# Dividing three more pairs of forget heads ahead of their turns, a third causal addition on GpSimd, and the turns of head group A five steps earlier

## The chip, the cores and the metric

One core of one Trainium2 chip runs the whole program. The metric is the device time of one execution in microseconds (us). The kernel before takes 1001.78 us, the median of three runs from 1001.54 to 1001.94. The engines are named as in the profile: PE (TensorE, matrix products), PEld (its weight loads), DVE (VectorE), ACT (ScalarE), POOL (GpSimd), SP (which issues most DMAs).

## The reference

Two layers work on 256 tokens of width 1024. Each layer is `h += 1/2 SwiGLU(norm(h))`, then `h += mixer(norm(h))`, then `h += 1/2 SwiGLU(norm(h))` again, all in float32. The mixer is where the change lies:

```python
proj = u @ w_in                       # 256 x 3792, split into the inputs of three head groups
aq = rope(rms(aq)); ak = rope(rms(ak))     # A: 4 query heads, one key/value head
iq, ik = rope(iq), rope(ik)                # A: indexer, 8 heads: the top 64 keys of each query
bq = rope(rms(bq)); bk = rope(rms(bk))     # B: 4 heads; with 256 tokens plain causal attention
cq, ck = rms(cq), rms(ck)                  # C: 8 heads
log_f = log_sigmoid(cf + forget_bias); c = cumsum(log_f)
s = q @ k.T / 8 (+ c_q - c_k in group C); masked softmax(s) @ v
o_c = o_c * sigmoid(cg)
out = concat(o_a, o_b, o_c) @ w_out
```

## The kernel before

Every float32 weight is split into a high and a low part (`wh`, `wl`), and a product is made of three PE products of parts. ACT makes `wh` (line 126), DVE makes `wl = raw - wh` (line 130); `W.pump()` asks for both of the next unit, `W.high()` and `W.low()` for one of them. Eight units are held at most, so the splits run ahead of PE.

The mixer's projection goes in chunks (`iq, ib, b, a, ck, cq, cv, cg`) of four units each. After each unit PE's instructions of one **step** stand in the program (12 products of 128x512), and `run_side()` then emits whatever has been put down for that step with `at_step(n, ...)`. In this way attention's small work is laid between the projection's products. Engines work through their own lists in order; what another engine must have made first is waited for. `A_ROOT`, `A_TURN`, `SUMS_STEP` and their like are such step numbers. A fraction counts for the next whole step: 21.3 is emitted after step 22, and 28.5 after step 29.

For group A, `a_norm` (at `A_ROOT`, step 22) takes the sums of squares on DVE, raises them to -1/2 on POOL (`y_a`, line 351), and scales the key head on POOL (`akd`, line 720). POOL has four things in a row there: `y_ck` and two scalings of `cka` (asked for at step 21), then `y_a` and the two `akd`. `a_turn` (at `A_TURN`) then turns the four query tiles `aqr` and the two `akd` on PE into PSUM (line 970), and ACT copies them to `aT`. `cumsum` turns the log gates `lf` on PE (line 905) and sums them on DVE; `sums_out` and `sums_in` send the sums through DRAM to every partition (`tab`, `laterkT`, `laterlater`), and `causal_part` adds the causal mask to them.

A pair of heads goes through `scores` (s, PE), `masks` (m, DVE: adds the mask and finds the row's extreme), `exps` (e, ACT), `roots` (n, DVE: reciprocals of the row sums), `flip` (F or f, PE: turns the 12 blocks of probabilities by products with the identity, line 180), `spread` (y: copies the turned blocks from PSUM to SBUF, half on DVE or ACT and half on ACT, line 193), `values` (v, PE) and `outT` (o). There are two ways to divide by the row sums. Pairs in `divided` scale the probabilities themselves before the flip (`divide`, words D or d, two instructions for a head). The others spread the reciprocals over a tile (`wide`, line 1112), turn that too with four more PE instructions, copy it with the blocks, and multiply afterwards. A letter string gives the order: `EARLY` after step 30, `AC_ORDER` after the projection. In it pairs 0 and 1 are group A, pairs 2 to 5 are group C; `h`, `r`, `p`, `x` stand for the output projection with `w_out`, and `j` is `W.low()`.

Names in rows: `ps_gu` and `ps_acc` are the two sets of four PSUM banks, `xhl` the normalized input in two parts, `oh`/`ol` and `ohl` the heads' outputs in two parts, `pT` turned probabilities, `cT` turned queries, keys and gates of group C.

Of the kernel before, what the change touches and what calls it, by code (L numbers as in the profile page):

```python
# [10 lines left out]
F32 = mybir.dt.float32  # L11
# [3 lines left out]
ALU = mybir.AluOpType  # L15
# [3 lines left out]
P = 128  # L19
S = 256  # L20
D = 1024
# [5 lines left out]
TOPK = 64  # L27
# [10 lines left out]
WARM = 6  # L38
BRIDGE = 3
P_BUFS = 4  # L40
EARLY = "S Q q m0 e0 m1 e1 m2 e2 b0 b1 m3 j B0 B1 e3"
AC_ORDER = """
    h0 n0 d0 C n1 d1 d2 d3 T c0 F0 k0 F1 y0 y1 c1 k1 s2 v0 v1 m4 m5 g o0 o1 e4 e5 s3 s4
    h1 m6 m7 w2 e6 e7 l q q n2 n3 w3 m8 m9 h2 h3
    F2 f3 y2 y3 s5 v2 v3 e8 e9 m10 m11 e10 e11 o2 o3 n4 j
    r0 r1 n5 j F4 F5 y4 y5 h4 j v4 v5 o4 o5 j
    p h5 h6 h7 Z r2 N p r3 p r4 p M x2 p x3 p
"""
B_TURN, A_ROPE, B_STEP, A_ROOT, A_TURN, SUMS_STEP, TOP_STEP, A_STEP = 18, 18, 20, 21.3, 28.5, 21, 15, 30


CHUNKS = [
# [102 lines left out]
def kernel(ctx: ExitStack, tc: tile.TileContext, x, ffn1_norm, ffn1_w_gate, ffn1_w_up, ffn1_w_down,  # L155
# [10 lines left out]
    at = ctx.enter_context(tc.tile_pool(name="at", bufs=1))  # L166
# [5 lines left out]
    V, A, G, T = nc.vector, nc.scalar, nc.gpsimd, nc.tensor  # L172

    def bank(tag):
        return psum.tile([P, 512], F32, name="ps_" + tag, tag=tag)
# [6 lines left out]
    def turned(ps, dst, copies):  # L182
        for e, copy in enumerate(copies):
            d = dst[..., 64 * e:64 * e + 64]
            n = 64
            for k in d.shape[1:-1]:
                n *= k
            src = ps[e][:, :n]
            if len(d.shape) == 3:
                src = src.rearrange("p (b j) -> p b j", j=64)  # L190
            else:
                src = src.rearrange("p (a b j) -> p a b j", a=d.shape[1], j=64)
            copy(d, src)
# [4 lines left out]
    def tmp(n):  # L198
        return tp.tile([P, 512], F32, name="tmp", tag="tmp")[:, :n]
# [39 lines left out]
    W = Weights(tc, raw_pool, split_pool)  # L239
# [89 lines left out]
    causal = cp.tile([P, 3 * P], F32, name="causal")  # L329
# [12 lines left out]
    def mm3(o, lhs, rhs, start, stop):  # L342
        mm(o, lhs[0], rhs[0], start, False)
        mm(o, lhs[0], rhs[1], False, False)
        mm(o, lhs[1], rhs[0], False, stop)
# [344 lines left out]
    def mixer(l, norm, nxt):  # L690
        side, count = [], itertools.count()
        step = [0]

        def at_step(n, fn):
            side.append((n, next(count), fn))

        def run_side():
            due = sorted(x for x in side if x[0] <= step[0])
            for x in due:
                x[2]()  # L700
            side[:] = [x for x in side if x[0] > step[0]]
# [47 lines left out]
        st = {}  # L749
# [44 lines left out]
        def post_ib(ps):  # L794
# [10 lines left out]
            for t in range(2):  # L805
                x = small[t][:, None, 0:64]
# [24 lines left out]
                A.activation(la, la, AF.Ln, bias=1.0)  # L831
                A.activation(small[0][:, 0:1], ones[:, 0:1], AF.Exp)

            at_step(SUMS_STEP - 3, log_sigmoid)
            def forget():
                V.scalar_tensor_tensor(lf, fg, 0.0, la, op0=ALU.min, op1=ALU.subtract)

            at_step(SUMS_STEP - 2, forget)
            st["ikT"] = at.tile([P, 1, S], F32, name="ikT", tag="qs")

            def turn_ik():
# [42 lines left out]
                V.match_replace(out=st["score"][t], in_to_replace=m8, in_values=st["score"][t], imm_value=-3e38)  # L884

            def amask_begin():
                st["amask"] = at.tile([P, 3 * P], F32, name="amask", tag="amask")
                G.tensor_copy(st["amask"][:TOPK, 0:P], causal[:TOPK, 0:P])

            at_step(A_STEP - 4, amask_begin)  # L890

            def amask():
                am, score = st["amask"], st["score"]
                for d, x in ((am[:, P:], score[1]), (am[TOPK:, :P], score[0][TOPK:])):
                    V.tensor_scalar(d, x, -2e38, NEG, op0=ALU.is_gt, op1=ALU.mult)

            at_step(A_STEP - 0.5, amask)

            for r in range(TOPK // 8):
                at_step(TOP_STEP + 2 * r, lambda: topk(1))  # L900
# [20 lines left out]
                    nc.sync.dma_start(to, bass.AP(tensor=src.tensor, offset=src.offset + h * S,  # L921
                                                    ap=[[0, P], [S, k], [1, n]]))

            at_step(SUMS_STEP + 1, cumsum)
            at_step(SUMS_STEP + 3, sums_out)
            at_step(SUMS_STEP + 5, sums_in)
            for i in range(2):
                at_step(A_STEP - 2, lambda i=i: causal_part(i))

        def causal_part(i):  # L930
            x = st["first"][:, 2 * i:2 * i + 4] if i % 2 == 0 else st["later"][i // 2][:, :, 1]
            (V if i > 1 else G).tensor_tensor(x, x, causal[:, None, 0:P].to_broadcast([P, 4, P]), op=ALU.add)

        def post_a(ps):
            ss = sm.tile([P, 2, 5], F32, name="ssa", tag="ss")
# [40 lines left out]
        def post_b(ps):  # L976
# [34 lines left out]
            def qk_b(kind, h):  # L1011
                return st["bT"][:, h // 2 * 2], st["bT"][:, h // 2 * 2 + 1]

            st["B"] = run_heads([("B", h) for h in range(4)], qk_b, lambda i, fn: at_step(B_STEP + i, fn))

        c_ss = at.tile([P, 2, 2, 8], F32, name="c_ss", tag="c_ss")
# [35 lines left out]
        def tanh():  # L1052
            ps, hr = st.pop("cg"), st["hr"]
            sg = at.tile([P, 2, 512], F32, name="sg", tag="sg")
            for t in range(2):
                A.activation(sg[:, t], ps[t], AF.Tanh, scale=hr[:, t:t + 1])
            st["sg"] = sg
            for _ in range(2):
                bank("gu")


        def run_heads(hs, qk, emit=None):
            pj, pt, op, sums, bs, wide, flipped, gated, high = {}, {}, {}, {}, {}, {}, {}, {}, {}
            divided = range(2)
            blocks = ((slice(0, P), slice(0, P), slice(0, P)), (slice(P, 3 * P), slice(P, S), slice(0, S)))
            tag = "acc" if emit else "gu"

# [65 lines left out]
            def spread(p):  # L1133
                both = pp.tile([P, 8, P], F32, name="pT", tag="pT", bufs=2)
                kind, h = hs[2 * p]
                turned(flipped.pop(p), both[:, :6] if p in divided else both,
                       (A.copy if emit else V.tensor_copy, A.copy))
                pt[p] = [both[:, 3 * e:3 * e + 3].rearrange("p a b -> p (a b)") for e in range(2)]
                gated[p] = both[:, 6:8].rearrange("p a b -> p (a b)")
                if kind == "C":  # L1140
                    o = st["gate"][:, h // 2]
                    if p not in divided:
                        o = tmp(S)
                        G.tensor_tensor(o, gated[p], st["gate"][:, h // 2], op=ALU.mult)
                    gated[p] = o
# [36 lines left out]
            if emit is None:  # L1182
                return scores, masks, exps, roots, divide, flip, spread, values, outT
# [10 lines left out]

        hs = [("A", h) for h in range(4)] + [("C", h) for h in range(8)]
        scores, masks, exps, roots, divide, flip, spread, values, outT = run_heads(hs, qk_ac)

        def c_T(ps, src, g, at):
# [5 lines left out]
        def both_scores(_):  # L1204
# [8 lines left out]
            for p in range(2):  # L1213
                b_values(p, st["keys"][p][:, S:])

        todo = dict(S=both_scores, D=divide, d=lambda i: divide(i, V), s=scores, m=masks, e=exps, n=roots, F=flip, y=spread, v=values, o=outT,
                    Q=lambda _: W.high(), q=lambda _: W.high(), j=lambda _: W.low(),
                    b=lambda p: st["B"][1](p), B=lambda p: st["B"][2](p), T=lambda _: tanh(), w=causal_part)

        def do(text):  # L1220
            for word in text.split():
                todo[word[0]](int(word[1:] or 0))

        at_step(A_STEP, lambda: do(EARLY))

        oT = {}
        posts = dict(ib=post_ib, a=post_a, b=post_b, ck=post_ck, cq=post_cq, cv=post_cv, cg=post_cg)
        index_queries()
        for name, cols in CHUNKS[1:]:
            n = sum(c[1] for c in cols)  # L1230
            ps = [bank("gu") for _ in range(2)]
            for u in range(4):
                w = W.take()
                for kk in range(2):
                    k = 2 * u + kk
                    for t in range(2):
                        ts = slice(t * P, (t + 1) * P)
                        mm3(ps[t][:, :n], (norm.h[:, k, ts], norm.l[:, k, ts]), [v[:, kk] for v in w],
                            k == 0, k == KT - 1)
                step[0] += 1  # L1240
                run_side()
                if step[0] < A_STEP and step[0] != 8:
                    W.pump()
            posts[name](ps)
            if step[0] == 8:
                W.pump(2)
# [70 lines left out]
        def norm_out(_):  # L1317
# [5 lines left out]
            for t in range(2):  # L1323
# [3 lines left out]
                    p=lambda _: W.pump(), Z=residuals, N=norm_T, M=norm_out)  # L1327
# [23 lines left out]
    for l in range(DEPTH):  # L1351
        norm = ffn(norm, lambda: Norm(1, l), lambda: before_mixer(l), l == 0)
        norm = mixer(l, norm, lambda: Norm(2, l))
        norm = ffn(norm, (lambda: Norm(0, l + 1)) if l + 1 < DEPTH else None)
# [37 lines left out]
```

## Time and profile before

| what | value |
|---|---|
| median of the runs | 1001.78 us |
| the profiled execution's own time | 1001.55 us |
| its span, first to last instruction | 999.8 us |
| PE busy | 995.5 us |
| DVE, ACT, POOL busy | 799.3, 597.4, 162.0 us |

The time outside the span is 1.75 us. A profile's row of PE shows a pipelined product: its length is longer than the time until the next can start, so starts are compared, not lengths. The two mixers run from about 189 to 321 us and from 684 to 816 us; the second repeats the first 494.9 us later, so rows of the first stand for both.

### The profile page before, as it was taken

The page shows a single profiled execution, that of the slowest core. Times are in us where ns is not written, and L with a number is a line of the kernel's source. Part 1 is how long each engine was busy: PE and PEld are TensorE (multiplying, and loading weights), DVE is VectorE, ACT ScalarE, POOL GpSimd, SP SyncE. Part 2 cuts the span into 40 slices and gives each one's busy share as a digit, 9 for nine tenths or more (in the row PEclk, how much of TensorE's full clock was granted, in tenths as well). Part 3 has the DMA queues.
Part 4 walks back from the last instruction along what each step waited for, and adds up shares of the span by engine and source line. Part 5 has one row for each costly group of instructions (what it writes and reads, how often), then busy time and mean ns, then how long its engine had stood idle before and what let it go on. Part 6 is the DMA issues. An engine that isn't in the chain of part 4 may idle for free.

```text
span 999.8 us, 15219 instructions
## 1 busy us (share of the span) xinstructions
PE 995.5 (100%) x5692; PEld 856.5 (86%) x5692; DVE 799.3 (80%) x1482; ACT 597.4 (60%) x1118; POOL 162.0 (16%) x188
## 2 busy tenths in 40 slices
PE   9999999999999999999999999999999999999998
PEld 8888888888878888888888888889888788888887
DVE  5978778789998777777888777787899977777775
ACT  6655555597786555555465555556968765555552
POOL 2003000058812000000000020001677210000000
PEclk9999999999999999999999999999999999999999
DMA  9865647475725555555655655565566164464731
GB/s 291 274 224 160 224 156 238 129 238 188 230 87 169 173 164 193 187 195 196 199 169 176 207 183 198 185 208 166 192 211 232 58 208 159 140 238 148 232 128 43
DMA packets 133498, 184.80 MB, mean 185 GB/s; under 512 B 7152, under 2 KB 106800, under 8 KB 133424
## 3 DMA queue, kind: packets, MB, share of 16 engines
q1 hardware_dynamic: 133392, 183.82, 56.2%
q8 instruction: 45, 0.74, 0.3%
q14 instruction: 29, 0.24, 0.1%
q10 hardware_dynamic: 32, 0.01, 0.0%
HBM read 182.75 MB, written 1.06 MB: 184 GB/s over the span
## 4 chain that ended last, share of the span: by engine, by line
PE 98%; DMA 1%; SPq 0%; ACT 0%; issue 0%; DVE 0%
PE ps_gu L340 66%; PE ps_acc L340 30%; PE ps_acc L180 1%; DMA raw<-in_ffn_w_up_dram 1%; PE ps_acc L375 1%; PE ps_gu L180 1%; SPq L100 0%; SPq L225 0%; PE ps_gu L375 0%; PE ps_acc L970 0%; ACT wh L126 0%; PE ps_acc L402 0%; PE ps_acc L844 0%; PE ps_acc L905 0%; DVE trunk L419 0%
## 5 line engine op out<-in xcount | busy, mean ns | idle before, releaser
L130 DVE TENSOR_TENSOR wl<-raw,wh 128x1024 fp32r<-128x1024 f32 (+2 forms) x342 | 421.6, 1240 | 27.1 <-ACT wh L126 27.1
L126 ACT CAST wh<-raw 128x1024 fp32r<-128x1024 f32 (+2 forms) x341 | 341.2, 1037 | 14.4 <-PE ps_acc L340 7.7
L340 PE MATMUL ps_gu<-xhl,wh 128*128 128x512 f32 (+1 forms) x1472 | 347.6, 388 | 0.2 <-ACT wh L126 0.2
L340 PEld LDWEIGHTS ps_gu<-xhl,wh 128*128 128x128 f32 x1472 | 272.5, 188 | 54.4 <-ACT wh L126 0.7
L340 PEld LDWEIGHTS ps_gu<-xhl,wl 128*128 128x128 f32 x1472 | 187.5, 191 | 4.1 <-DVE wl L521 0.2
L340 PE MATMUL ps_gu<-xhl,wl 128*128 128x256 f32 (+1 forms) x1472 | 190.3, 282 | 0.0
L484 DVE TENSOR_TENSOR tmp<-ps_gu,tmp 128x256 f32<-128x256 f32 x176 | 72.8, 422 | 109.3 <-ACT tmp L483 109.0
L340 PE MATMUL ps_acc<-wh,hh 128*128 128x512 f32 (+1 forms) x352 | 137.3, 390 | 0.0
L340 PE MATMUL ps_acc<-wl,hh 128*128 128x512 f32 (+1 forms) x352 | 137.0, 389 | 0.0
L340 PE MATMUL ps_acc<-wh,hl 128*128 128x512 f32 (+1 forms) x352 | 136.6, 388 | 0.0
L340 PE MATMUL ps_gu<-wh,xhl 128*128 128x512 f32 (+2 forms) x448 | 133.4, 375 | 0.0
L483 ACT COPY tmp<-ps_gu 128x256 f32<-128x256 f32 x176 | 63.4, 371 | 92.1 <-PE ps_gu L340 91.9
L498 ACT CAST hh<-tmp 128x256 fp32r<-128x256 f32 x80 | 32.6, 407 | 120.2 <-DVE tmp L495 120.2
L340 PEld LDWEIGHTS ps_gu<-wh,xhl 128*128 128x128 f32 x448 | 82.5, 188 | 14.1 <-issue 1.7
L490 ACT ACTIVATE tmp<-tmp 128x256 f32<-128x256 f32 x88 | 36.9, 419 | 82.7 <-DVE tmp L488 82.5
L340 PE MATMUL ps_gu<-wl,xhl 128*128 128x512 f32 (+2 forms) x224 | 83.2, 372 | 0.0
L351 POOL TENSOR_TENSOR y_n<-msq,minus_half 128x2 f32<-128x2 f32 x6 | 7.0, 1174 | 441.9 <-DVE msq L350 441.9
L340 PEld LDWEIGHTS ps_acc<-wh,hl 128*128 128x128 f32 x352 | 66.1, 188 | 13.9
L340 PEld LDWEIGHTS ps_acc<-wh,hh 128*128 128x128 f32 x352 | 66.2, 188 | 12.6
L340 PEld LDWEIGHTS ps_acc<-wl,hh 128*128 128x128 f32 x352 | 66.3, 188 | 12.3 <-DVE wl L130 0.2
L340 PEld LDWEIGHTS ps_gu<-wl,xhl 128*128 128x128 f32 x224 | 42.2, 188 | 5.9
L508 DVE TENSOR_TENSOR tmp<-tmp,rb 128x256 f32<-128x256 f32 x88 | 37.7, 428 | 3.0
(237 smaller groups left out, 901.5 us busy)
## 6 DMA issues: line engine op xcount, KB each, us to landing
raw<-in_ffn_w_down_dram SPq DMA_DIRECT2D x44, 1024.0 KB, 5.0
raw<-in_ffn_w_gate_dram SPq DMA_DIRECT2D x42, 1024.0 KB, 6.9
raw<-in_ffn_w_up_dram SPq DMA_DIRECT2D x42, 1024.0 KB, 7.8
raw<-in_w_in_dram SPq DMA_DIRECT2D x24, 1024.0 KB, 5.1
raw<-in_w_out_dram SPq DMA_DIRECT2D x8, 1024.0 KB, 5.0
raw<-in_w_in_dram SPq DMA_DIRECT2D x4, 768.0 KB, 5.0
raw<-in_w_in_dram SPq DMA_DIRECT2D x4, 656.0 KB, 4.2
raw<-in_ffn_w_gate_dram SPq DMA_DIRECT2D x3, 512.0 KB, 7.5
```

The source lines that it names most:

```text
L126: self.nc.scalar.copy(hv, src)
L130: (engine or self.nc.vector).tensor_tensor(lv, self.srcs[self.n_low], hv.bitcast(F32), op=ALU.subtract)
L180: T.transpose(b[:, 64 * i:64 * i + 64], src[r], ident[r, r])
L340: T.matmul(o, l, r, start=start, stop=stop, skip_group_check=True)
L351: G.tensor_tensor(y, dst, minus_half[:, :n], op=ALU.pow)
L375: T.transpose(ps[:, i, t * P:(t + 1) * P], trunk[:, t, (2 * mp + i) * P:(2 * mp + i + 1) * P], ident)
L483: A.copy(o, ps[:, 1])
L484: V.tensor_tensor(o, ps[:, 0], o, op=ALU.add)
L490: A.activation(th, t_, AF.Tanh, scale=0.5)
L498: (V.tensor_copy if late else A.copy)(hh, t_)
L508: V.tensor_tensor(t_, t_, norm.rb, op=ALU.mult)
```

## The change

Six things change. (1) `divided` grows from two pairs to five: pairs 2, 3 and 4 (forget heads) now have their probabilities divided before the flip, head 4 on POOL (new word G), heads 5 to 9 on DVE (d); their reciprocals are no longer spread, turned and copied, and the gate is multiplied in directly. (2) `a_turn` moves from step 29 to step 24, `cumsum` from step 22 to 24, `sums_out` from 24 to 26, `sums_in` from 26 to 27. (3) The mask of group A and the causal additions move from steps 28 and 30 to the word `a` in `EARLY`; three additions instead of two go to POOL, and they read a copy of the mask that DVE makes in `amask`. (4) In `spread`, group B's copies go to DVE and ACT instead of ACT twice. (5) Step 29 asks for a `wh` only, and its `wl` follows as `j` in `EARLY`. (6) `AC_ORDER` is reordered around this; the second `j` of its fourth line stands two places later, and mask 9 after the copies of pairs 2 and 3.

```diff
-EARLY = "S Q q m0 e0 m1 e1 m2 e2 b0 b1 m3 j B0 B1 e3"
+EARLY = "S j a Q q m0 e0 m1 e1 m2 e2 b0 b1 m3 j B0 B1 e3"
...
-    h1 m6 m7 w2 e6 e7 l q q n2 n3 w3 m8 m9 h2 h3
-    F2 f3 y2 y3 s5 v2 v3 e8 e9 m10 m11 e10 e11 o2 o3 n4 j
-    r0 r1 n5 j F4 F5 y4 y5 h4 j v4 v5 o4 o5 j
+    h1 m6 m7 n2 G4 d5 e6 e7 l q q n3 d6 d7 w3 m8 h2 h3
+    F2 f3 y2 y3 m9 s5 v2 v3 e8 e9 m10 m11 e10 e11 o2 n4 d8 d9 o3 n5
+    r0 r1 j F4 F5 y4 y5 h4 j v4 v5 o4 o5 j j
...
-B_TURN, A_ROPE, B_STEP, A_ROOT, A_TURN, SUMS_STEP, TOP_STEP, A_STEP = 18, 18, 20, 21.3, 28.5, 21, 15, 30
+B_TURN, A_ROPE, B_STEP, A_ROOT, A_TURN, SUMS_STEP, TOP_STEP, A_STEP = 18, 18, 20, 21.3, 24, 24, 15, 30
...
             def amask():
                 am, score = st["amask"], st["score"]
-                for d, x in ((am[:, P:], score[1]), (am[TOPK:, :P], score[0][TOPK:])):
+                for d, x in ((am[:, P:3 * P], score[1]), (am[TOPK:, :P], score[0][TOPK:])):
                     V.tensor_scalar(d, x, -2e38, NEG, op0=ALU.is_gt, op1=ALU.mult)
-
-            at_step(A_STEP - 0.5, amask)
+                V.tensor_copy(am[:, 3 * P:], causal[:, 0:P])
+                for i in range(3):
+                    causal_part(i)
+
+            st["mask"] = amask
...
-            at_step(SUMS_STEP + 1, cumsum)
-            at_step(SUMS_STEP + 3, sums_out)
-            at_step(SUMS_STEP + 5, sums_in)
-            for i in range(2):
-                at_step(A_STEP - 2, lambda i=i: causal_part(i))
+            at_step(SUMS_STEP, cumsum)
+            at_step(SUMS_STEP + 2, sums_out)
+            at_step(SUMS_STEP + 3, sums_in)
...
-            (V if i > 1 else G).tensor_tensor(x, x, causal[:, None, 0:P].to_broadcast([P, 4, P]), op=ALU.add)
+            late = i > 2
+            mask = causal[:, 0:P] if late else st["amask"][:, 3 * P:]
+            (V if late else G).tensor_tensor(x, x, mask[:, None].to_broadcast([P, 4, P]), op=ALU.add)
...
-            divided = range(2)
+            divided = range(5)
...
-                       (A.copy if emit else V.tensor_copy, A.copy))
+                       (V.tensor_copy, A.copy))
...
-                if step[0] < A_STEP and step[0] != 8:
+                if step[0] < A_STEP - 1 and step[0] != 8:
                     W.pump()
+                if step[0] == A_STEP - 1:
+                    W.high()
```

On PE, the turns of group A stood at the end of step 29 in the kernel before, 84 products after the turns of the log gates:

```order
L340 MATMUL ps_gu<-wh,xhl 128x512
L970 MATMUL ps_acc<-ident,aqr 128x128 [waits Pool_49] x2
L970 MATMUL ps_acc<-ident,aqr 128x128 x2
L970 MATMUL ps_acc<-ident,akd_2514 128x128 [waits Pool_49]
L970 MATMUL ps_acc<-ident,akd_2515 128x128 [waits Pool_49]
L340 MATMUL ps_gu<-wh,xhl 128x512
```

In the changed kernel both sets of turns stand together on PE, at the end of step 24:

```order
L340 MATMUL ps_gu<-wh,xhl 128x512
L908 MATMUL ps_acc<-ident,lf 8x128 [waits DVE_49]
L908 MATMUL ps_acc<-ident,lf 8x128
L973 MATMUL ps_acc<-ident,aqr 128x128 [waits DVE_49,Pool_49]
L973 MATMUL ps_acc<-ident,aqr 128x128 [waits Pool_49]
L973 MATMUL ps_acc<-ident,aqr 128x128 x2
L973 MATMUL ps_acc<-ident,akd_2514 128x128 [waits DVE_49,Pool_49]
L973 MATMUL ps_acc<-ident,akd_2515 128x128 [waits Pool_49]
L340 MATMUL ps_gu<-wh,xhl 128x512 [waits Activation_49]
```

The turns of `akd` still wait for POOL, and everything that PE has to do later stands behind them. The turns of `lf` came down by two steps (24 products), those of `aqr` and `akd` went up by five.

On POOL, the rows that make `akd` stand in the changed kernel exactly as they stood, behind the scaling of `cka`:

```order
L351 TENSOR_TENSOR y_ck<-c_ss,minus_half 128x16 [waits DVE_49]
L720 TENSOR_TENSOR cka_130<-cka_130,y_ck 128x512 [waits Activation_49,Pool_49]
L720 TENSOR_TENSOR cka_131<-cka_131,y_ck 128x512 [waits Activation_49]
L351 TENSOR_TENSOR y_a<-ssa,minus_half 128x10 [waits DVE_49]
L720 TENSOR_TENSOR akd_2514<-ak_2512,y_a 128x128 [waits PE_49,Pool_49]
L720 TENSOR_TENSOR akd_2515<-ak_2513,y_a 128x128 [waits PE_49]
```

Nothing on POOL moved ahead of them or away from ahead of them; what it does later (three additions, the division of head 4) follows.

On PE again, the flips of pairs 2 and 3 and the scores of pair 5 in the kernel before, in AC_ORDER (`tmp` is the spread reciprocal):

```order
L180 MATMUL ps_gu<-ident,p 128x64 x3
L180 MATMUL ps_gu<-ident,tmp 128x64 [waits DVE_49]
L180 MATMUL ps_gu<-ident,tmp 128x64 x3
L180 MATMUL ps_acc<-ident,p 128x64 [waits Activation_49] x2
L180 MATMUL ps_acc<-ident,p 128x64 x10
L180 MATMUL ps_acc<-ident,tmp 128x64 [waits DVE_49]
L180 MATMUL ps_acc<-ident,tmp 128x64 x3
L340 MATMUL ps_gu<-cT 128x128 [waits DVE_49] x2
```

And the end of the same stretch on PE in the changed kernel:

```order
L180 MATMUL ps_acc<-ident,p 128x64 [waits DVE_49]
L180 MATMUL ps_acc<-ident,p 128x64
L180 MATMUL ps_acc<-ident,p 128x64 [waits DVE_49]
L180 MATMUL ps_acc<-ident,p 128x64 x3
L340 MATMUL ps_gu<-cT 128x128 [waits DVE_49]
L340 MATMUL ps_gu<-cT 128x128 [waits Activation_49]
```

The turns of `tmp` are gone. The second product of the scores now waits for ACT: its PSUM bank is the one that ACT's copy of pair 2 (line 193) sets free, where before both banks came free by masks on DVE.

## Rows read from the trace of the kernel before

**Rows 1.** The page: span, and busy time of each engine.

```profile
span 999.8 us, 15219 instructions
PE 995.5 (100%) x5692; PEld 856.5 (86%) x5692; DVE 799.3 (80%) x1482; ACT 597.4 (60%) x1118; POOL 162.0 (16%) x188
```

**Rows 2.** All waits of PE: total us, times, longest.

```profile
PE ps_gu L340 <- POOL minus_half L219: 1.0, 1, 1.0
PE ps_gu L340 <- ACT wh L126: 0.2, 1, 0.2
```

**Rows 3.** Timeline of PE, end of step 22: start, us, then the instruction.

```profile
250.34 0.38 PE L905 MATMUL ps_acc<-ident,lf 128*8 128x128 f32 x2
250.47 0.48 PE L340 MATMUL ps_gu<-wh,xhl 128*128 128x512 f32 x1
```

**Rows 4.** Timeline of PE, the turns of group A.

```profile
269.63 0.60 PE L970 MATMUL ps_acc<-ident,aqr 128*128 128x128 f32 x4
270.07 0.38 PE L970 MATMUL ps_acc<-ident,akd 128*128 128x128 f32 x2
```

**Rows 5.** Timeline of POOL, 251 to 259 us; [idle before, and who ended it].

```profile
251.16 2.91 POOL L351 TENSOR_TENSOR y_ck<-c_ss,minus_half 128x16 f32<-128x16 f32 x1 [4.68 <-DVE c_ss L350]
254.15 2.09 POOL L720 TENSOR_TENSOR cka<-cka,y_ck 128x512 f32<-128x512 f32 x2
256.20 1.95 POOL L351 TENSOR_TENSOR y_a<-ssa,minus_half 128x10 f32<-128x10 f32 x1
258.23 0.76 POOL L720 TENSOR_TENSOR akd<-ak,y_a 128x128 f32<-128x128 f32 x2
```

**Rows 6.** Line 351: ns min/median/max, first and last start in us.

```profile
L351 POOL TENSOR_TENSOR y_n<-msq,minus_half x6: 702/1201/1612, 16.0 to 819.7; 128x2 f32<-128x2 f32 x6
L351 POOL TENSOR_TENSOR y_a<-ssa,minus_half x2: 1947/1947/1947, 256.2 to 751.1; 128x10 f32<-128x10 f32 x2
```

**Rows 7.** Windows after the last product: length, busy by engine, then PEclk, DMA.

```profile
996.75:998.75 2.00, 0.00 (x0) 0.00 (x0) 0.42 (x1) 0.00 (x0) 0.00 (x0) 1.00 0.33 115
998.76:999.80 1.04, 0.00 (x0) 0.00 (x0) 0.00 (x0) 0.00 (x0) 0.00 (x0) 0.50 0.00 0
```

**Rows 8.** Timeline of PE, the same four turns early and later.

```profile
4.12 1.11 PE L537 MATMUL ps_acc<-ident,trunk 128*128 128x128 f32 x4
...
7.50 0.60 PE L537 MATMUL ps_acc<-ident,trunk 128*128 128x128 f32 x4
```

**Rows 9.** Timeline of PE, after the flips of pairs 2 and 3.

```profile
295.47 0.29 PE L180 MATMUL ps_acc<-ident,tmp 64*128 64x64 f32 x4
295.59 0.33 PE L340 MATMUL ps_gu<-cT 64*128 64x128 f32 x2
```

**Rows 10.** Timeline of PE, keys of group C turned after step 30.

```profile
275.31 0.60 PE L180 MATMUL ps_acc<-ident,cka 64*128 64x64 f32 x8
275.84 0.44 PE L340 MATMUL ps_acc<-pT,vB 128*64 128x256 f32 x2
```

**Rows 11.** Timeline of ACT, the first copy of pair 2.

```profile
295.38 0.59 ACT L193 COPY pT<-ps_gu 128x512 f32<-128x512 f32 x1 [0.79 <-PE ps_gu L180]
```

**Rows 12.** ACT by line and shape: busy us, mean ns.

```profile
L193 ACT COPY pT<-ps_gu 128x384 f32<-128x384 f32 x4 | 1.7, 484 | 0.0
```

**Rows 13.** Timeline of PE, second product with the seventh unit of w_out.

```profile
306.71 0.40 PE L340 MATMUL ps_acc<-wl,ohl 128*128 128x512 f32 x1
```

**Rows 14.** Timeline of DVE there, two splits.

```profile
303.31 1.44 DVE L130 TENSOR_TENSOR wl<-raw,wh 128x1024 fp32r<-128x1024 f32 x1
...
305.72 1.70 DVE L130 TENSOR_TENSOR wl<-raw,wh 128x1024 fp32r<-128x1024 f32 x1
```

**Rows 15.** Lines 1120 and 1112 on DVE, ns min/median/max.

```profile
L1120 DVE TENSOR_SCALAR p<-p,sums x16: 260/318/354, 282.5 to 779.5; 128x128 f32<-128x128 f32 x8, 128x256 f32<-128x256 f32 x8
L1112 DVE COPY tmp<-sums x8: 293/294/294, 292.2 to 795.1; 128x256 f32<-128x256 f32 x8
```

**Rows 16.** Windows, attention after the projection: length, PE, PEld, DVE, ACT, POOL busy.

```profile
276.00:310.00 34.00, 34.00 (x312) 26.32 (x311) 30.55 (x97) 24.65 (x75) 8.76 (x9) 1.00 0.31 94
```

More of the change, by code (lines that the diff above doesn't have):

```diff
@@ L832, in log_sigmoid @@
                 A.activation(small[0][:, 0:1], ones[:, 0:1], AF.Exp)
-            at_step(SUMS_STEP - 3, log_sigmoid)
+            at_step(18, log_sigmoid)
             def forget():
                 V.scalar_tensor_tensor(lf, fg, 0.0, la, op0=ALU.min, op1=ALU.subtract)
-            at_step(SUMS_STEP - 2, forget)
+            at_step(19, forget)
             st["ikT"] = at.tile([P, 1, S], F32, name="ikT", tag="qs")
@@ L886, in amask_begin @@
             def amask_begin():
-                st["amask"] = at.tile([P, 3 * P], F32, name="amask", tag="amask")
+                st["amask"] = at.tile([P, 4 * P], F32, name="amask", tag="amask")
                 G.tensor_copy(st["amask"][:TOPK, 0:P], causal[:TOPK, 0:P])
@@ L1214, in both_scores @@
                 b_values(p, st["keys"][p][:, S:])
-        todo = dict(S=both_scores, D=divide, d=lambda i: divide(i, V), s=scores, m=masks, e=exps, n=roots, F=flip, y=spread, v=values, o=outT,
+        todo = dict(S=both_scores, D=divide, d=lambda i: divide(i, V), G=lambda i: divide(i, G), s=scores, m=masks, e=exps, n=roots, F=flip, y=spread, v=values, o=outT,
                     Q=lambda _: W.high(), q=lambda _: W.high(), j=lambda _: W.low(),
-                    b=lambda p: st["B"][1](p), B=lambda p: st["B"][2](p), T=lambda _: tanh(), w=causal_part)
+                    b=lambda p: st["B"][1](p), B=lambda p: st["B"][2](p), T=lambda _: tanh(), w=causal_part,
+                    a=lambda _: st["mask"]())
         def do(text):
```

## The prediction

> **What bounds the kernel now.** I read the page's busy times first, then the waits of PE, then PE's timeline at every place that the change touches, then POOL and DVE beside it. PE is busy 995.5 of 999.8 us, DVE 80%, ACT 60%, POOL 16% [rows 1]. All of PE's waits come to 1.2 us, and 1.0 of that is the program's first instruction [rows 2]. So PE's list is the time: an instruction taken out of it is gained in full, a wait put into it is lost in full, and it is never caught up, since PE has no idle time to catch up in. Work on another engine costs nothing unless PE then waits for it.
>
> **The turns of group A: the main term.** The six turns wait for POOL's two `akd`. In the kernel before there are 84 products between the turns of the log gates and these [rows 3, 4]: 269.63 - 250.47 = 19.16 us, 0.228 for a product. In the changed kernel both sets of turns stand after step 24, 24 products behind the place where `lf` was turned. PE gets there at 250.34 + 24 x 0.228 = 255.81. The two `lf` take 0.13 (250.34 to 250.47), the four `aqr` 0.44 (269.63 to 270.07), the first `akd` 0.07 (half of the 0.13 of [rows 3], a pair of like turns). The second `akd` would start at 256.45.
>
> POOL's list there is unchanged, and its beginning hangs on a DVE operation (`c_ss`) that the change doesn't move. It raises `y_ck` from 251.16, scales `cka` until 256.24, raises `y_a` until 258.15 and ends the second `akd` at 258.23 + 0.76 = 258.99 [rows 5]. PE therefore waits 258.99 - 256.45 = 2.54 us, nearly all of it at the first `akd`. The second layer has the same `y_a`, 1947 ns at 751.1, 494.9 later than in the first [rows 6]. Both layers: 5.1 us. Spans on POOL are rough, so I bound it: a `y_a` as short as the shortest power of line 351, 0.70 [rows 6], would still leave 2.54 - 1.25 = 1.3 a layer, 2.6 in all. Upward I allow 0.2 a layer for the signal to PE.
>
> Behind the waiting turn PE has the rest of the projection, steps 25 on, all of it. On ACT the copies to `aT` wait for these turns, and behind them ACT's own splits. Eight units of split weights lie ahead, so I put no further wait there; DVE and POOL gain time by the pause.
>
> **The clock.** A pause can cost more than itself. After its last product PE does nothing; the granted clock stood at 1.00 for the first 2.00 us and then at 0.50 (1.2 GHz) [rows 7]. The wait here is of that length: some 2.2 us without a product, a turn, and 0.35 more. What slow running costs shows at the start: four turns of `trunk` took 0.91 from 4.12 (the next product comes at 5.03), and 0.35 from 7.50 [rows 8]; I read that as the lower level, though no record of the clock marks it there. PE began at 1.0, so it was slow for some 4.2 us, and at half speed 2.1 of that were lost. A fall thus costs between 0 and 2.1 us in each layer. I take 1.6, one fall in one of the two layers, because the one pause in the trace that can be compared brought the clock down at about this length.
>
> The Trainium skill (TensorE: Matmul & The Clock Gate, section "Why this matters for your kernels") has a rule that speaks against this term: only pauses longer than the one it names bring the clock back down between bursts, and ours would be short enough. By it the sum loses 1.6. The trace does not quite agree, since its clock was down after 2.00 us; I follow the trace, and keep the other as a rival.
>
> **What goes from PE.** Pairs 2, 3 and 4 no longer turn their reciprocals. One pair's four turns took 0.12 us (295.47 to 295.59) [rows 9]; three pairs 0.36 a layer. The eight turns of `cka` after step 30 took 0.53 (275.31 to 275.84) [rows 10], where two such sets of four should take 0.24: PE stood there for group B's copies on ACT. With DVE sharing these, between 0 and 0.29 is gained; I take half, 0.15. Together -0.5 a layer.
>
> **Small new waits.** (a) The second product of `s5` now takes the bank that ACT's copy of pair 2 frees. That copy began at 295.38 [rows 11]. Without the 0.12 of `tmp` before it, it begins at 295.26; six blocks instead of eight take 0.484 (a copy of this shape) [rows 12], so it ends at 295.74. PE is there at 295.59 - 0.24 + 0.1 = 295.45 at the latest (two pairs' turns gone). That is 0.3, with the signal 0.4. Below, 0, if ACT gets to it sooner; above 0.6, if it takes as long as the one before, 0.59. (b) The `wl` of the last units of `w_out` are split one place later. PE needs the seventh at 306.71 [rows 13]; DVE's split at that place ran from 305.72 to 307.42 [rows 14], 0.7 late. With the shorter 1.44 of the split before, and DVE there some 0.2 earlier, it is 0.3. I take 0.3, from 0 to 0.7. Together +0.7, so the small terms are +0.2 a layer, 0.4 in all, from -0.5 to +0.8 a layer.
>
> **What DVE, POOL and the DMAs take over.** DVE divides five heads: 10 x 0.318 = 3.2 us, minus three copies of reciprocals at 0.294 [rows 15], 2.3 more; one addition and part of three copies less makes it about 1.5. In that stretch DVE was busy 30.55 of 34.00 us and POOL 8.76 [rows 16]: there is 3.45 to hide it in, and head 4 goes to POOL. I cost it at nothing. If the cover fails, the flips wait: up to 1.5 us a layer, less what (a) and (b) already count. The sums' DMAs leave later, but their first readers, the causal additions, move back as well, from steps 28 and 30 to after step 30. Nothing.
>
> **The sum.** The profiled execution took 1001.55 us in all. 1001.55 + 5.1 (wait) + 0.4 (small terms) + 1.6 (clock) = 1008.65. It was 0.23 below the median, so against the median that is 1008.9.
>
> **The rivals.** (1) The clock stays up. For it: the pause is broken by a turn, and is hardly longer than 2.00 us. Against it: the fall after the last product [rows 7]. It gives 1008.9 - 1.6 = 1007.3. (2) POOL is in time, and nothing is slower: if the second `akd` is ready before 256.45, the main wait and the clock's share are gone, and 1001.78 + 0.4 = 1002.2 is left, or 1000.8 when the small waits too fail to come (-0.5 x 2). For it: POOL was idle 4.68 us before `y_ck` [rows 5], so an earlier `c_ss` would bring it forward, and DVE no longer has the log gates' sums to do two steps earlier. Against it: it needs 2.5 us on POOL, and the order before `c_ss` is the same. The point that decides is `akd` ending at 256.45. (3) The second half becomes late as well: DVE's 1.5 us meet the flips, ACT's copies the scores, and (b) is at its 0.7. 1.4 a layer on top: 1008.9 + 2.8 = 1011.7. For it: PE has no slack anywhere [rows 2]. Against it: DVE's 3.45 us.
>
> **How the numbers follow.** Forecast 0.58, clock up 0.22, POOL in time 0.08, later second half 0.12. The likeliest gives 1008.9. The range, 1004.6 to 1012.0, takes in the first rival, a short `y_a` with the clock up (1001.78 + 2.6 + 0.4 = 1004.8) and the third rival; it leaves out the second and the tails. About 2.0 us, 0.2%, is what a measurement can tell from no change. The second rival at 1002.2 is no change; only its best form with a gain elsewhere would be faster: 0.02 faster, 0.06 same, 0.92 slower.
>
> **What would show it.** In the profile after: one wait of PE for POOL's `akd` at the turns of group A in each layer, 2.3 to 2.7 us long; a dip of the granted clock behind at least one of them, with products at twice their spacing; turns of `tmp` down from 32 to 8; a wait of PE for ACT's copy of pair 2, 0.3 to 0.6; a wait for a late `wl` in the output projection, 0 to 0.7. If the rows of POOL are where they were and PE shows no wait there, the main step is wrong; if waits of PE in the second half come to more than 1.5 a layer, DVE's cover is.

## The result and the profile after

The changed kernel takes 1008.8 us, the median of five executions from 1008.53 to 1010.68, against 1001.78 before: a ratio of 1.0077, 95% interval 1.0064 to 1.0091. The forecast was 1008.9. The profile shows that the place and the size of its main term were right, and that two smaller terms were wrong by nearly the same amount in opposite directions.

The page of the changed kernel, span and busy times, against [rows 1]:

```profile
span 1006.8 us, 15179 instructions
PE 997.1 (99%) x5668; PEld 856.0 (85%) x5668; DVE 802.0 (80%) x1500; ACT 595.6 (59%) x1114; POOL 163.8 (16%) x188
```

All its waits of PE (total us, times, longest), against [rows 2]:

```profile
PE ps_acc L973 <- POOL akd L720: 4.2, 2, 2.1
PE ps_gu L340 <- POOL minus_half L219: 1.0, 1, 1.0
PE ps_acc L340 <- DVE wl L130: 0.9, 2, 0.4
PE ps_gu L340 <- ACT wh L126: 0.3, 1, 0.3
```

The span is 7.0 us longer. Two kinds of waits are new on PE: for POOL's `akd` at the turns of group A, once in each layer, and for DVE's `wl` (line 130). The profiled execution itself took 1008.53 us.

POOL in the changed kernel over the stretch of [rows 5], with the idle time before a row in brackets:

```profile
251.30 2.91 POOL L351 TENSOR_TENSOR y_ck<-c_ss,minus_half 128x16 f32<-128x16 f32 x1 [4.68 <-DVE c_ss L350]
254.29 2.08 POOL L720 TENSOR_TENSOR cka<-cka,y_ck 128x512 f32<-128x512 f32 x2
256.34 1.95 POOL L351 TENSOR_TENSOR y_a<-ssa,minus_half 128x10 f32<-128x10 f32 x1
258.37 0.76 POOL L720 TENSOR_TENSOR akd<-ak,y_a 128x128 f32<-128x128 f32 x2
```

And PE at the turns there, against [rows 3, 4], with the second layer's `akd` at the end:

```profile
255.88 0.38 PE L908 MATMUL ps_acc<-ident,lf 128*8 128x128 f32 x2
256.10 0.60 PE L973 MATMUL ps_acc<-ident,aqr 128*128 128x128 f32 x4
258.82 0.68 PE L973 MATMUL ps_acc<-ident,akd 128*128 128x128 f32 x2 [2.12 <-POOL akd L720]
259.26 0.48 PE L340 MATMUL ps_gu<-wh,xhl 128*128 128x512 f32 x1
...
757.13 0.69 PE L973 MATMUL ps_acc<-ident,akd 128*128 128x128 f32 x2 [2.11 <-POOL akd L720]
```

POOL's rows stand where they stood, 0.14 us later. PE comes to the turns five steps earlier and waits for the same `akd`. The bracket counts only from the modelled end of `aqr`; what the pause costs is the time by which the product behind it is late.

The turns of `cka` and the values of group B stand against [rows 10]; the flips of pairs 2 and 3 now end at the first scores of pair 5, against [rows 9]; and the place of [rows 13] has a wait before it. PE there:

```profile
277.95 0.41 PE L180 MATMUL ps_acc<-ident,cka 64*128 64x64 f32 x8
278.29 1.09 PE L340 MATMUL ps_acc<-pT,vB 128*64 128x256 f32 x10
...
297.75 0.33 PE L340 MATMUL ps_gu<-cT 64*128 64x128 f32 x1
...
309.01 0.40 PE L340 MATMUL ps_acc<-wh,ohl 128*128 128x512 f32 x1
309.84 0.51 PE L340 MATMUL ps_acc<-wl,ohl 128*128 128x512 f32 x1 [0.44 <-DVE wl L130]
```

At 275.84 [rows 10] PE was at the values of group B; in the changed kernel it is there at 278.29, 2.45 late. At the scores of pair 5 it is 297.75 - 295.59 = 2.16 late: the turns of reciprocals are gone, and that is 0.29 us where 0.24 (pairs 2 and 3) were forecast by then. At the product with the seventh unit's `wl` it is 309.84 - 306.71 = 3.13 late. So 0.97 us came back between the scores of pair 5 and this product, and some 0.4 more after it, to about 3.5 us for the layer; two layers make the 7.0 of the span.

The granted clock behind the pause, by windows (length, then PE, PEld, DVE, ACT and POOL busy, granted clock, DMA share, GB/s):

```profile
259.20:262.60 3.40, 3.40 (x16) 2.82 (x17) 3.02 (x8) 3.40 (x8) 2.67 (x3) 1.00 0.80 299
```

It stayed at 1.00 (2.4 GHz), in this execution. Of the five executions three had a mean clock of 1.000 over the span (1008.5 to 1008.8 us) and two 0.998 (1010.15 and 1010.68 us).

### The profile page after: what moved, and what is told of

It is laid out like the page before. It is cut to its first block, busy times and chain, and to the rows that moved or that the text cites. A ratio compares the mean times of both kernels' runs of the same rounds, so it can differ in the third digit from the quotient of the medians.

```text
span 1006.8 us, 15179 instructions
## 1 busy us (share of the span) xinstructions
PE 997.1 (99%) x5668; PEld 856.0 (85%) x5668; DVE 802.0 (80%) x1500; ACT 595.6 (59%) x1114; POOL 163.8 (16%) x188
## 4 chain that ended last, share of the span: by engine, by line
PE 94%; POOL 2%; DVE 1%; issue 1%; DMA 1%; SPq 0%; ACT 0%; DVEq 0%; POOLq 0%; ACTq 0%
PE ps_gu L340 62%; PE ps_acc L340 29%; DMA raw<-in_ffn_w_up_dram 1%; PE ps_acc L375 1%; PE ps_acc L180 1%; DVE wl L130 1%; PE ps_gu L180 0%; POOL y_a L351 0%; DVE score L870 0%; ACT wh L126 0%; POOL y_ck L351 0%; POOL y_bk L351 0%; POOL aqr L714 0%; POOL aqr L715 0%; SPq L100 0%
```

## The experiments

The theory after the result: the pause for `akd` costs some 2.55 us in each layer and is paid in full; the clock falls behind it in some executions only; the rest of the change is slower by itself, by late splits and a late PSUM bank, and not faster. The rivals: the pause is only an early part of a lateness that would come out elsewhere, or DVE's added divisions are what costs.

### The turns by themselves

Run e1 undoes only the place of the turns:

```diff
-... A_ROOT, A_TURN, SUMS_STEP, ... = 18, 18, 20, 21.3, 24, 24, 15, 30
+... A_ROOT, A_TURN, SUMS_STEP, ... = 18, 18, 20, 21.3, 28.5, 24, 15, 30
```

> The changed kernel with the turns of group A back after step 29 and everything else of the change kept. Theory (the pause at the turns is paid in full and once; the rest of the change costs about 1.9 us by late splits and one late PSUM bank): 1008.8 - 5.1 = 1003.7 us, PE shows no wait for akd, 0.9 us of waits for wl stay, no execution shows a granted clock under 1.000. Rival (the pause gives other engines time, and without it the same lateness comes back in the second half of the mixer): 1006 us or more, with new waits of PE at the flips or scores.

Measured 1004.48 us (1004.0 to 1004.94, eight executions), ratio to before 1.0028 [1.0017, 1.0038]. PE has no wait for `akd`, and all executions show a clock of 1.000. The theory's value is missed by 0.8 us, the rival's by 1.5: most of the pause is paid, a part of it comes back.

Run e2 makes that one edit in the kernel before (`A_TURN` 24 instead of 28.5):

> The kernel before with one edit: the turns of group A after step 24 instead of 29. Theory: 1001.8 + 5.1 = 1006.9 us in executions in which the clock stays up, 1.4 to 1.9 more in those in which it falls once (some of the five, their mean clock at 0.998). Rival (the cost is that of the added divisions and additions): 1002 us.

Measured 1009.62 us (1006.84 to 1009.73), so the rival, 1002 us, falls. The executions say how: 1006.84 us with a mean clock of 1.000, 1008.79 with 0.998, and 1009.62 to 1009.73 three times with 0.996. So by the one execution in which the clock stayed up, the turns alone cost 5.1 us, where the whole change costs 7.0 (1008.53 to 1008.8 with the clock up); the medians are alike only because the clock fell more often here. The profiled execution is one of the last three. PE at the pause in it:

```profile
258.61 0.69 PE L970 MATMUL ps_acc<-ident,akd 128*128 128x128 f32 x2 [2.08 <-POOL akd L720]
...
260.07 0.62 PE L340 MATMUL ps_gu<-wl,xhl 128*128 128x512 f32 x1
260.49 1.06 PE L340 MATMUL ps_gu<-wh,xhl 128*128 128x512 f32 x2
261.34 0.63 PE L340 MATMUL ps_gu<-wl,xhl 128*128 128x512 f32 x1
```

The clock there, by windows as above:

```profile
255.00:258.80 3.80, 1.72 (x10) 1.20 (x8) 3.73 (x15) 3.43 (x10) 3.72 (x5) 1.00 0.01 2
259.10:262.40 3.30, 3.30 (x11) 2.65 (x12) 3.23 (x9) 3.30 (x7) 2.45 (x3) 0.65 0.89 297
262.50:266.00 3.50, 3.50 (x14) 2.77 (x14) 3.40 (x11) 3.50 (x6) 2.77 (x4) 0.86 0.56 188
```

From 260.07 the starts are 0.42 to 0.43 us apart, where 0.23 is usual: half speed (1.2 GHz). It comes after the pause, when PE is working again, and it goes again by itself. One fall costs 1008.79 - 1006.84 = 1.95 us, two cost 2.8, so 1.4 each; the two slower executions of the changed kernel were 1.4 and 2.0 above the other three. The estimate of 1.6 for one fall holds; how often it falls was the open part.

Run e4, in the kernel before, makes the pause twice as long (`A_TURN` 23):

> The kernel before with the turns of group A after step 23, to make the pause twice as long (5.3 us in each layer). Theory for the waits: 1001.8 + 10.5 = 1012.3 us plus the clock. If falls of the clock come by chance with pauses of this kind, and more surely with longer ones, nearly every execution shows a mean clock of 0.997 or less and 1.4 to 2 us more for each fall: 1015 to 1016 us. Rival (the two slow executions of the changed kernel have nothing to do with the clock): 1012.3 us with a clock of 1.000.

Measured 1015.88 us, four executions: 1014.80 and 1015.24 with a clock of 0.997, 1016.52 and 1016.87 with 0.993. None kept the clock. PE's wait in the profiled one:

```profile
258.57 0.83 PE L970 MATMUL ps_acc<-ident,akd 128*128 128x128 f32 x2 [4.80 <-POOL akd L720]
```

And the windows behind it:

```profile
259.00:262.00 3.00, 3.00 (x9) 2.42 (x9) 2.93 (x9) 3.00 (x7) 2.14 (x3) 0.50 0.83 279
262.00:266.00 4.00, 4.00 (x13) 3.10 (x13) 2.91 (x9) 2.89 (x6) 2.90 (x3) 0.65 0.58 202
```

Against the 1012.3 us of the waits alone, the clock took 2.5 to 4.6 us. So a pause near 2.5 us brought the clock down in some executions, and one of 5 in all four; the rival, that the slower executions have nothing to do with the clock, falls.

The Trainium skill (TensorE: Matmul & The Clock Gate, section "Why this matters for your kernels") would let a pause of the shorter kind pass. In e2 it did so in one execution of five, and in the changed kernel in three of five. The measurement decides: a pause shorter than the one named there is not safe.

### Where the pause is made

Run e3 moves the turns of the changed kernel one step later (`A_TURN` 25):

> The changed kernel with the turns of group A one step later, after step 25. Theory: PE comes 2.73 us later, 0.2 us after POOL's second akd is ready, so there is no wait: 1003.7 us, as with the turns after step 29, clock at 1.000 throughout. Rival (the early place itself hurts, by the copies on ACT and the PSUM banks held there): between 1005 and 1008 us.

Measured 1004.69 us, ratio 1.0029 [1.0018, 1.0041]. It equals e1 within 0.2 us, so the early place itself doesn't hurt: one step is the whole price. In e3 POOL's last `akd` is ready at 259.29 and PE turns the first at 259.48, without a wait.

Run e5 keeps the turns where the change has them and puts POOL's work in the other order instead (`A_ROOT` 20.2):

```diff
-... A_ROOT, A_TURN, SUMS_STEP, ... = 18, 18, 20, 21.3, 24, 24, 15, 30
+... A_ROOT, A_TURN, SUMS_STEP, ... = 18, 18, 20, 20.2, 24, 24, 15, 30
```

> The changed kernel with the root of group A put down one step earlier (step 21), so that on POOL y_a and the two akd stand ahead of y_ck and the cka; the turns stay after step 24. Theory (the pause is POOL's order at the turns and nothing else): akd is ready some 2 us before PE comes, no wait of PE for akd, clock at 1.000 in all executions, 1004.5 us as with the turns one step later. Rival (POOL has too much to do there, whatever the order): PE then waits somewhere else, 1006 us or more.

Measured 1004.37 us (1004.03 to 1004.73), no wait for `akd`, and a mean clock of 1.000, once 0.999 as in some executions of the kernel before. POOL in e5:

```profile
250.82 1.96 POOL L351 TENSOR_TENSOR y_a<-ssa,minus_half 128x10 f32<-128x10 f32 x1 [4.28 <-DVE ssa L350]
252.86 0.76 POOL L720 TENSOR_TENSOR akd<-ak,y_a 128x128 f32<-128x128 f32 x2
...
253.82 2.93 POOL L351 TENSOR_TENSOR y_ck<-c_ss,minus_half 128x16 f32<-128x16 f32 x1
```

And PE there:

```profile
255.84 0.38 PE L908 MATMUL ps_acc<-ident,lf 128*8 128x128 f32 x2
256.06 0.60 PE L973 MATMUL ps_acc<-ident,aqr 128*128 128x128 f32 x4
256.49 0.38 PE L973 MATMUL ps_acc<-ident,akd 128*128 128x128 f32 x2
256.63 0.47 PE L340 MATMUL ps_gu<-wh,xhl 128*128 128x512 f32 x1
```

From the first `lf` to the product behind the turns PE takes 256.63 - 255.84 = 0.79 us here, and 259.26 - 255.88 = 3.38 in the changed kernel: the pause costs 2.59 a layer, 5.2 in all. Yet e5 is only 4.4 below the changed kernel. In e1, e3 and e5 PE loses some 0.2 us at the scores of group A in each layer, and in the changed kernel it doesn't. DVE and PE there in e5:

```profile
274.39 1.01 DVE L193 COPY pT<-ps_acc 128x384 f32<-128x384 f32 x2
274.67 1.03 PE L340 MATMUL ps_acc<-aT 64*128 64x128 f32 x7
```

One of these products waits for the first of DVE's copies of group B's blocks (over at 274.93) and starts at 274.99; in the kernel before, where ACT makes the copies, it starts at 274.69. The values of group B then start at 276.08, 0.24 behind the kernel before. In the changed kernel the pause gave DVE time for these copies; in e8 and e11, where ACT makes them again, the loss is gone. So a part of the rival is true: 0.8 us out of 5.2 come back by the medians. By the two traces it is 1.0, and 0.83 of it here: e5 is ahead of the changed kernel by 2.63 us before these products and 2.21 behind them, by 4.72 and 4.31 in the second layer.

### What the rest of the change costs

All these runs but e10 have the turns after step 25, so e3's 1004.69 us stands for "the change without its pause". Run e6 puts the splits earlier:

```diff
-    ... o2 n4 d8 d9 o3 n5
-    r0 r1 j F4 F5 y4 y5 h4 j v4 v5 o4 o5 j j
+    ... o2 n4 d8 d9 o3 n5 j
+    r0 r1 j F4 F5 y4 y5 h4 j v4 v5 o4 o5 j
```

> The run with the turns after step 25 (1004.7 us), and the two j of AC_ORDER back at their old places. Theory (the late wl is the place of the split): the waits of PE for wl in the output projection go, 0.9 to 1.0 us in each layer: 1002.8 us. Rival (DVE is late by its load, and the place doesn't matter): 1004.2 us or more, with the waits still there.

Measured 1003.93 us, ratio 1.0021 [1.0013, 1.0030]. The waits for `wl` are gone, as the theory said, but less than half of the gain comes, 0.76 us of 1.9: PE waits 0.4 us in each layer for DVE's copy of pair 4 instead.

Run e7 puts mask 9 back where it was:

```diff
-    ... w3 m8 h2 h3
-    F2 f3 y2 y3 m9 s5 ...
+    ... w3 m8 m9 h2 h3
+    F2 f3 y2 y3 s5 ...
```

> The run with the turns after step 25 (1004.7 us), and mask 9 ahead of the copies of pairs 2 and 3 as it was. Theory (the second scores product of pair 5 waits for the bank of ACT's copy): 0.4 us less in each layer, 1003.9 us, and the gap between the first two products of s5 falls from 0.44 to 0.16 us. Rival (DVE gets to mask 9 and the copies in either order, and one of them is late): 1004.7 us, the gap only moves to the flips or values.

Measured 1003.79 us, ratio 1.0019 [1.0010, 1.0027], as the theory said (1003.9). ACT's copy of pair 2 in the changed kernel, and then PE at `s5` in e7, where the same eight products start at 295.54 and the values already at 296.34:

```profile
297.66 0.48 ACT L193 COPY pT<-ps_gu 128x384 f32<-128x384 f32 x1 [0.65 <-PE ps_gu L180]
```

```profile
295.54 0.87 PE L340 MATMUL ps_gu<-cT 64*128 64x128 f32 x8
296.34 0.87 PE L340 MATMUL ps_gu<-pT,va 128*64 128x256 f32 x8
```

In the changed kernel these eight products take 1.36 us instead of 0.87: the second, in the other bank, starts at 298.19, when ACT's copy is over (298.14), 0.44 us behind the first. That is term (a) of the sum.

Run e8 takes both edits and gives group B's copies back to ACT:

```diff
-                       (V.tensor_copy, A.copy))
+                       (A.copy if emit else V.tensor_copy, A.copy))
```

> The run with the turns after step 25, with both of these edits, and group B's copies on ACT twice again; the divisions and the moved masks, additions and sums stay. If the parts add up: 1004.7 - 1.9 - 0.8 - 0.3 = 1001.7 us, the same as the kernel before: the 0.7 of the turns that went is eaten by what else came. If the divisions pay in full: 1001.0 us. If DVE's load is what costs: 1003 us or more, with waits for DVE that move about.

Measured 1003.48 us, ratio 1.0016 [1.0007, 1.0025]: the third of the three cases, DVE's load by the look of it. PE is 0.23 us ahead of the kernel before at the scores of pair 5 (295.36 against 295.59), so the turns that went were gained; then it waits. PE and DVE in e8:

```profile
304.14 0.65 PE L340 MATMUL ps_gu<-pT,va 128*64 128x256 f32 x4 [0.82 <-DVE pT L193]
```

```profile
299.67 0.18 DVE L1111 RECIPROCAL sums<-sums 128x4 f32<-128x4 f32 x1
...
300.09 3.44 DVE L130 TENSOR_TENSOR wl<-raw,wh 128x1024 fp32r<-128x1024 f32 x2
303.45 1.14 DVE L193 COPY pT<-ps_gu 128x384 f32<-128x384 f32 x2
```

Two splits stand in a row ahead of the copies. Is it the divisions of heads 8 and 9 that made them late? Run e9 leaves these out:

```diff
-            divided = range(5)
+            divided = range(4)
-    ... o2 n4 d8 d9 o3 n5 j
+    ... o2 n4 o3 n5 j
```

> The run with all three edits back (1003.5 us), and pair 4 no longer divided ahead of its flip: DVE loses the divisions of heads 8 and 9 (4 x about 0.25 to 0.3 us) and gets one copy of reciprocals (0.29); PE gets four turns (0.12). Theory (DVE is about 0.8 us late at the copies of pairs 4 and 5, because of those divisions): PE's wait for DVE's pT there, 0.8 us in each layer, goes or falls under 0.2: 1002.0 us. Rival (the additions, or the gate multiplied on DVE after the flips, make it late): the wait stays at 0.6 or more, 1003.5 us.

Measured 1004.19 us, ratio 1.0025 [1.0015, 1.0034]: slower still, and the wait is at 0.9 us. The theory falls. DVE in e9 shows why:

```profile
299.72 0.18 DVE L1111 RECIPROCAL sums<-sums 128x4 f32<-128x4 f32 x1 [0.92 <-ACT p L1105]
...
300.14 3.44 DVE L130 TENSOR_TENSOR wl<-raw,wh 128x1024 fp32r<-128x1024 f32 x2
```

Without the divisions DVE stands idle for 0.92 us at the reciprocals of pair 5, which wait for ACT's probabilities; the splits behind them begin at the same time as in e8. In the kernel before a split stood between the reciprocals of pair 4 and those of pair 5 (`n4 j r0 r1 n5 j`). The change moved `n5` ahead of it, and so did e6 to e9, whose `j` isn't quite at its old place for that reason.

Run e10 asks the same of the divisions alone, in the kernel before:

```diff
-    h1 m6 m7 w2 e6 e7 l q q n2 n3 w3 m8 m9 h2 h3
+    h1 m6 m7 w2 n2 G4 d5 e6 e7 l q q n3 d6 d7 w3 m8 m9 h2 h3
-            divided = range(2)
+            divided = range(4)
```

> The kernel before with one part of the change: pairs 2 and 3 divided ahead of their flips (head 4 on POOL, 5 to 7 on DVE), all else as it was. If the four turns of a pair are all that changes on PE's path: 2 pairs x 0.12 x 2 layers = 0.5 us less, 1001.2 us. If DVE has no room for 6 x 0.32 - 2 x 0.29 = 1.3 us between 284 and 295 us: waits of PE for DVE at the flips or scores, 1002.5 us or more.

Measured 1002.43 us, ratio 1.0009 [1.0000, 1.0018]. That is close to the second case. PE comes to `s5` 0.36 us earlier than before (295.23 against 295.59; 0.14 of it stems from before the attention) and loses 0.44 there, because DVE, which still has two additions of 0.7 us in that stretch, ends mask 9 only at 295.56; some 0.2 us a layer more go in the output projection, and what takes them was not traced. The move of an addition to POOL seems to be what the divisions need here; it was not tried by itself.

Run e11 is e8 with a split between the two pairs of reciprocals again, and e12 the same with four pairs divided:

```diff
-    ... o2 n4 d8 d9 o3 n5 j
-    r0 r1 j F4 ...
+    ... o2 n4 j d8 d9 o3
+    r0 r1 n5 j F4 ...
```

> The run with all three edits back and five pairs divided (1003.5 us), and the first of its two splits put between the reciprocals of pairs 4 and 5, where the kernel before has it (in the earlier runs both splits stood behind the reciprocals of pair 5). Theory now (DVE stands idle there until ACT's probabilities of pair 5, and a split must fill that gap): PE's wait for DVE's pT falls from 0.8 to 0.2 us or less in each layer, 1002.0 us or less. Rival (the divisions of heads 8 and 9 make DVE late): the wait stays above 0.5, 1003 us.

> The same with four pairs divided. Theory: no wait for pT either, four turns (0.12 us) in each layer more than with five pairs: 1002.0 to 1002.2 us. If heads 8 and 9 do weigh on DVE, this is the faster of the two by 0.5 us or more.

Measured 1000.90 us for e11 (1000.75 to 1001.86, eleven executions), ratio 0.9991 [0.9982, 1.0000], and 1001.38 us for e12, ratio 0.9996 [0.9987, 1.0005]. DVE in e11, and its copies of pair 4:

```profile
299.08 1.19 DVE L130 TENSOR_TENSOR wl<-raw,wh 128x1024 fp32r<-128x1024 f32 x1
300.19 1.00 DVE L1123 TENSOR_SCALAR p<-p,sums 128x128 f32<-128x128 f32 x4
...
301.89 1.21 DVE L130 TENSOR_TENSOR wl<-raw,wh 128x1024 fp32r<-128x1024 f32 x1
303.03 1.14 DVE L193 COPY pT<-ps_gu 128x384 f32<-128x384 f32 x2
```

PE waits neither for `pT` nor for `wl` any more. The divisions of all five heads fit on DVE (e12, without those of heads 8 and 9, is the slower of the two by 0.48 us); what did not fit was the order. e11 is the fastest of all kernels here, 0.85 us below the kernel before, with an interval that just reaches no difference; by the traces PE gains 0.7 us against it between 14 us and the end, and the rest is the spread of the executions.

The order does two things here, and the expectations name only one. A split ahead of `n5` fills DVE's idle time. It also takes less time itself, in step with POOL's work: POOL makes the low half of the heads' outputs (`ol`, line 1183), in e8 and then in e11:

```profile
300.01 2.43 POOL L1183 TENSOR_TENSOR ol<-tmp,oh 128x256 fp32r<-128x256 f32 x2 [7.28 <-ACT oh L1175]
```

```profile
301.09 0.74 POOL L1183 TENSOR_TENSOR ol<-tmp,oh 128x256 fp32r<-128x256 f32 x1 [7.32 <-ACT oh L1175]
302.04 1.66 POOL L1183 TENSOR_TENSOR ol<-tmp,oh 128x256 fp32r<-128x256 f32 x1 [0.22 <-ACT oh L1175]
```

In e8 both splits begin while POOL is at this, and take 3.44 us together, 1.76 each. In e11 one runs without POOL and the other begins between the two rows: 1.19 and 1.21 us. All fourteen profiles agree: the 3808 splits of this shape that no POOL instruction overlaps took 1.19 to 1.23 us, the 204 in which POOL only starts later took the same, and the 70 that begin while POOL makes `ol` or `ohl` took 1.70 to 1.80. Counted from the first product of `s5` (295.36 in e8, 296.42 in e11), DVE comes to the copies 1.48 us earlier in e11 than in e8 (6.61 us behind it against 8.09): 1.04 of this are the shorter splits, and only the rest is idle time filled. Between e9 and e12 it is the other way: 1.56 us, of which the splits are 0.47.

## Why the prediction was right, and where it was not

**The main wait: right.** 2.54 us a layer were forecast from POOL's rows and 24 products; 2.59 were measured. POOL's rows stayed, POOL did not come in time, and 1.3, the lower bound, was not needed. That PE pays it in full held but for 0.8 us of 5.2 (e1, e3, e5): the pause gave DVE time that the rest of the change then needed. The text put such gains aside without a price.

**The clock: the size right, the count wrong.** One fall costs 1.4 to 2.0 us, 1.6 was taken. But the step "one fall in one of the two layers" failed for the median: three executions of five had none, two had one, and the dip named as a sign is not in the profiled execution. The step rested on one fall at the end of one execution, 2.00 us after the last product [rows 7]. That time is not fixed: in e7 the last product ends at 998.70, and the clock still stood at 1.00 3.0 us later:

```profile
998.80:1001.70 2.90, 0.00 (x0) 0.00 (x0) 0.37 (x1) 0.00 (x0) 0.00 (x0) 1.00 0.19 68
```

In e2, with nearly the same pause, it was the other way: four of five fell, three of them in both layers. Why the two kernels differ in this was not tried, and stays open. A price that is paid by chance belongs in the range and not in the likeliest time.

**The turns that went: right.** 0.29 us are seen between group B's values and the scores of pair 5, where two of the three pairs were to give 0.24; e11 gains 0.7 in two layers, the whole sum, when nothing else is late.

**Group B's copies: half right.** The gain at the turns of `cka` came: 0.34 us from their start to the values of group B, against 0.53 before, so 0.19 where 0.15 was taken. But without the pause DVE's share of the copies makes the scores of group A late by 0.2. That neighbour was not looked at.

**The bank of `s5`: right**, 0.4 forecast, 0.44 seen, and 0.9 us in two layers by e7.

**The late `wl`: the step that was mis-sized.** It was put at 0.3 us, with 0.7 as its bound; it costs 0.6 at the seventh unit and 0.3 more at the eighth. The sum saw one split as late and took the shorter duration for it, 1.44. In the profile after two splits stand in a row from 308.04, together 3.42 us long, 1.75 each, with POOL at work on `ohl`:

```profile
308.04 3.42 DVE L130 TENSOR_TENSOR wl<-raw,wh 128x1024 fp32r<-128x1024 f32 x2
307.96 2.42 POOL L1183 TENSOR_TENSOR ohl<-tmp,ohl 128x256 fp32r<-128x256 f32 x2 [0.94 <-ACT ohl L1175]
```

The first ends at 309.79 and PE goes on at 309.84; the second ends at 311.46 and PE goes on with the next unit's `wl` at 311.52. With 1.75 in place of 1.44 the forecast's own working gives the 0.6 of the seventh unit; the split of the eighth was not looked at.

**The sum.** The small terms come to about 1.8 us (7.0 less 5.2) instead of 0.4, the clock to 0 instead of 1.6 in the median. These errors cancel, and so 1008.9 against 1008.8 is closer than the working deserved: the first rival, the clock that stays up, is what most executions did, and a part of the third, a later second half, came with it.

**DVE at nothing: right for the work, wrong in the reason.** 3.45 us of idle time were set against 1.5 of new work. DVE did have the room (e11), but part of the idle time lay where it waited for ACT, and the order decided whether a split could use it and whether a split met POOL's work and took some 0.5 us longer.

## What to carry to other kernels

When PE has no slack, a turn or product moved earlier is worth nothing unless what it reads is ready there: read the end of the other engine's rows at the new place, and if it is late, swap that engine's order or move by the one step that is missing. An engine with idle time in a stretch can still be late there: see what ends its idle time, and put a piece of independent work right in front of that wait. Before taking an instruction's length from another row, see what the other engines did during that row: here the same split took 1.2 us or 1.75. A forecast with two small terms of opposite sign should be judged by its terms, not by its total.

## What the runs showed that was not expected

A pause of PE of about 2.5 us, with one of the turns inside it, brings the granted clock to half in some executions and not in others of the same kernel (two of five in the changed kernel, four of five in e2). In the profile of e2 the fall shows 1.5 us after PE has started again (258.61 to 260.07); in the pause of 5 us of e4 the clock is at 0.50 from 257.95 on, 0.6 us before PE starts again (258.57). So a kernel with such a pause has times that spread by 2 to 3 us (1008.5 to 1010.7, 1006.8 to 1009.7), while in each of the runs without it (e1, e3, e5 to e12) they lie within 0.4 to 1.1 us (e6: 1003.64 to 1004.23, e11: 1000.75 to 1001.86). Such a spread can itself be a sign of the pause.
